# Thirty-two of forty-two projection blocks by seven products, with attention moved behind them

## The chip, the cores and the metric

The kernel runs on one core of one Trainium2 chip. The core has TensorE (PE, with a queue of its own for weight loads, PEld), VectorE (DVE), ScalarE (ACT), GpSimd (POOL) and SyncE (SP), which here issues nearly all DMAs. The metric is the time of one execution on the device in microseconds. A profile is one execution taken apart by the hardware profiler. Line numbers (L216) are those of the kernel file.

## The reference: what is computed

One layer of a decoder for 1024 prompt rows and 32 sample rows (8 sequences of 4), width 1024, all in float32:

```python
h = layer_norm(ALPHA * x + 0.5 * swiglu(x, f1_w1, f1_w3, f1_w2), ln1_g, ln1_b)
z = h @ w_in + b_in                       # 1024 -> 5376: q, k, v (3 x 768), u, v (2 x 512), gates (2 x 1024)
...
for g, (window, dil) in enumerate(ATT_GROUPS):   # (128,1), (512,4), (2048,16), 4 heads of 64 each
    o, lse, nbuf = dilated_attn_prompt(qg, kg, vg, tab, window, dil)      # or ..._sample with the stored keys
att = combine_groups(outs, lses).astype(h.dtype)          # softmax over the three groups' lse
yb, vrows = sgu_branch(uv, sgu_ln_g, sgu_ln_b, sgu_ws, sgu_b)   # gelu, LN of v, 128x128 token mixing, u * mixed
mix = (jax.nn.sigmoid(ga) * (att @ w_oa) + jax.nn.sigmoid(gb) * (yb @ w_ob)) @ w_out
h = layer_norm(ALPHA * h + mix, ln2_g, ln2_b)
h = layer_norm(ALPHA * h + 0.5 * swiglu(h, f2_w1, f2_w3, f2_w2), ln3_g, ln3_b)
```

Besides the rows of h it returns the last keys and values of each group (prompt and sample) and the normalised v rows of the sample.

## The kernel before

Everything stands transposed: features on the 128 partitions, the 1056 rows (1024 + 32) along the free dimension, in `NC` = 4 chunks of `C` = 264. Weights come as blocks of 128 output features. Each float32 operand is split into a rounded part and a rest (`split`, L227 a cast on ACT, L228 a subtraction on DVE), and each product is three matmuls (`mm3`, recorded at L216). A dense block for one chunk (`dense8`) is 8 x 3 = 24 matmuls of 128x128 by 264 columns.

The kernel's stages are: the first half step (`ffn`), `project`, `mix`, the second half step. In a half step most blocks are not computed densely. `hidden` takes two weight blocks as a 2x2 matrix of halves (two blocks, two halves of the 1024 inputs) and the rows as a 2x2 matrix (two halves of the inputs; even and odd chunks), and gets the product by seven products of sums and differences (the Winograd form of Strassen's scheme) instead of eight. `spread` makes the sums of the rows (four for each pair of chunks, on DVE, with casts on ACT), `prep` those of the weights (four additions on POOL or DVE, then splits), `product` runs the 24 matmuls of one of the seven. The results add up in three pairs of PSUM banks (`banks`).

`project` computes the 26 blocks of q, k, v and of the two SGU halves densely, in the order `ZORDER`. The first three blocks run chunk by chunk, as the first layer norm delivers its chunks; each result stays in SBUF. With every third block a head pair of one group is complete, and its attention (`attend`) is put in a queue. `attend` transposes v, forms scores (L1055), adds the bias and finds the row's limit (L1063, DVE), takes exponentials with their sums (L1067, ACT), transposes them (L1078, copied by ACT at L1082) and multiplies with v (L1094). The stored keys and values of the sample are worked on by DVE in slabs of 16 positions (`sample`, L1233 to L1250). `combine` weights the three groups by way of DRAM (L1154 to L1182, tables mlD and cD). SGU follows (`sgu_norm`, `sgu_mix`). `mix` computes the 16 gate blocks (sigmoid, L1393), the products with w_oa and w_ob (`product` inside it, L1402), their sum (L1409), and then w_out (L1491).

The order of work is set by the program and by a planner that fixes each engine's order before the run. Three queues of generators hold work that runs in between: `bg`, `slow`, `mid`. `tick(n, m)` lets n steps of `bg`, m of `slow` and three of `mid` into the program after each block; `step` takes always the first generator of its queue. `urgent` moves PSUM reads ahead. `STEPS` holds the numbers of steps for each stage. SBUF is given out in slots: 37 of 4.1 KB per partition (`S`), 8 for split weights (`W`), 2 for raw weights (`R`), 6 small ones (`M`). PSUM has three banks `mm` and five `ax`. A tile waits until a slot of its kind is free.

Of the kernel before, what the change touches and what calls it, by code (L numbers as in the profile page):

```python
# [20 lines left out]
P = 128  # L21
D = 1024
# [28 lines left out]
PIECE = 16  # L51
# [3 lines left out]
STEPS = dict(lead=6, strassen=3, seven=2, out=2, project=2, gate=1, wout=3)  # L55
# [10 lines left out]
ZORDER = [s * 6 + 2 * g + hp for hp, g in HPG for s in range(3)] + [22, 23, 24, 25] + [18, 19, 20, 21]  # L66


class Trunk:
# [705 lines left out]
    def out(self, w2, i, mode, ready, between, load):  # L775
# [84 lines left out]
        for c in range(NC):  # L860
            early = 6 if c == 0 else 0
            if mode != "out":
                self.hold_normed(c)
                if c == 2:
                    self.early = [self.unit(self.a["wz"][n], slot=True, ahead=AFTER) for n in range(3)]
                    self.early = self.early, [self.held([P, NT]) for _ in range(3)]
# [55 lines left out]
    def project(self):  # L922
        nc = self.nc
        self.att = [None, None]
# [4 lines left out]
        self.jD = self.dp.tile([6, 64, 66], F32, name="jD")  # L929
        lns, self.lns = self.lns, {}  # L930
        self.A = self.normed
        ws, held = self.early
        tiles = dict(enumerate(held))
        load = lambda i: self.unit(self.a["wz"][i])
        self.vr = [None] * 4
        self.vn = None
        self.yb = [None] * 4

        def block(i, w, c):
            if c in lns:  # L940
                self.drain(lns.pop(c))
            nb = ZORDER[i]
            p = self.mm_tile()[:, :C]
            self.dense8(p, w, c)
            if i not in tiles:
                tiles[i] = self.S([P, NT])
            t = tiles[i]
            ctx = self.urgent()
            ctx.__enter__()
            b, sc, dil = self.bin(nb), 1.0, 1  # L950
            if nb < 18:
                s, g = nb // 6, (nb % 6) // 2
                if s == 0:
                    b, sc = self.qb[:, nb : nb + 1], -0.125
                dil = GROUPS[g][1]
            put = lambda o, x: nc.scalar.activation(o, x, AF.Identity, bias=b, scale=sc)  # L956
            c0, c1 = c * C, c * C + C
            if dil == 1:
                put(t[:, c0:c1], p)
            else:  # L960
                cut = min(c1, NP)
# [7 lines left out]
                if cut < c1:  # L969
                    put(t[:, NP:], p[:, cut - c0 :])  # L970
# [709 lines left out]
```

## Time and profile before

| | us |
|---|---|
| median of 3 runs (2200.23 to 2209.55) | 2204.38 |
| the profiled execution's own time | 2201.41 |
| its span, first to last instruction | 2199.5 |
| TensorE busy in it | 2168.9 |
| DVE busy | 1467.2 |
| ACT busy | 869.1 |
| POOL busy | 254.7 |

The granted TensorE clock was 0.996 of full speed over the span. In a row of instruction groups stand: line, engine, operation, written tile <- read tiles, form, count; then busy time in us and mean ns of one; then idle time of the engine before them and who ended it. The busy time of a group counts overlapping instructions once, so it may be smaller than count times mean. In a row of stretches stand the window, its length and each engine's busy time with the number of instructions that began in it.

### The profile page before, as it was taken

To read this page: it belongs to the slowest core of one execution; us is meant where nothing else is said; L and a number is where in the kernel's file an instruction comes from. 1 tells how busy PE (TensorE), PEld (TensorE's weight loads), DVE (VectorE), ACT (ScalarE), POOL (GpSimd) and SP (SyncE) were. 2 spreads that over 40 slices of the span, in tenths; PEclk is the share of its full clock that TensorE was granted. 3 is DMA by queue.
4 is the path that set the end of the run, shared out by engine and by line. 5 is a ranking of instruction groups with operands and counts; after the bars stand their busy time and mean duration, and the time that the engine had idled before them with its cause. 6 is when DMAs were issued, how large, how long until landed. Compare 5 with 4: busy or idle time off the path is not lost.

```text
span 2199.5 us, 42970 instructions
## 1 busy us (share of the span) xinstructions
PE 2168.9 (99%) x17593; PEld 2125.4 (97%) x17593; DVE 1467.2 (67%) x2465; ACT 869.1 (40%) x1647; POOL 254.7 (12%) x193
## 2 busy tenths in 40 slices
PE   9999999999999999999999999999999999999997
PEld 8999999999999999888999999998999999999997
DVE  8776776656789337557862624578677667656787
ACT  5444444421125544444354123246444444322124
POOL 0432332200000000000000000000333233100000
PEclk9999999999999999999999999999999999999999
DMA  4445445596954135344531312513545445596832
GB/s 158 146 139 179 171 161 183 186 378 258 348 205 155 69 103 184 96 155 157 195 109 68 111 48 79 180 69 112 175 156 185 171 159 178 197 366 250 313 103 80
DMA packets 136278, 370.33 MB, mean 168 GB/s; under 512 B 21056, under 2 KB 48432, under 8 KB 133392
## 3 DMA queue, kind: packets, MB, share of 16 engines
q1 hardware_dynamic: 135648, 367.04, 48.1%
q8 instruction: 138, 2.26, 0.4%
q10 hardware_dynamic: 432, 0.54, 0.1%
q14 instruction: 60, 0.49, 0.1%
HBM read 277.85 MB, written 135.86 MB: 188 GB/s over the span
## 4 chain that ended last, share of the span: by engine, by line
PE 92%; DVE 3%; DMA 2%; ACT 1%; issue 1%; ACTq 0%; SPq 0%; DVEq 0%
PE mm L216 49%; PE ax L216 39%; PE ax L1055 1%; PE ax L1094 1%; PE ax L1078 1%; DVE S L228 1%; DMA S<-kv 1%; DVE S L594 0%; DMA S<-cD 0%; PE ax L1361 0%; DMA S<-xc 0%; PE ax L583 0%; ACT S L227 0%; ACT S L602 0%; DVE S L523 0%
## 5 line engine op out<-in xcount | busy, mean ns | idle before, releaser
L216 PE MATMUL mm<-S,W 128*128 128x264 f32 x7224 | 936.7, 287 | 9.4 <-DVE S L858 4.9
L216 PEld LDWEIGHTS mm<-S,W 128*128 128x128 f32 x7224 | 899.6, 189 | 25.1 <-issue 11.0
L216 PE MATMUL ax<-S,W 128*128 128x264 f32 x4536 | 596.0, 284 | 0.0
L216 PEld LDWEIGHTS ax<-S,W 128*128 128x128 f32 x4536 | 570.0, 188 | 1.0 <-issue 1.0
L216 PE MATMUL ax<-S,S 128*128 128x264 f32 x2664 | 390.9, 285 | 0.0
L216 PEld LDWEIGHTS ax<-S,S 128*128 128x128 f32 x2664 | 351.2, 188 | 1.0 <-DVE S L228 0.6
L216 PE MATMUL mm<-S,S 128*128 128x264 f32 x2184 | 334.9, 286 | 4.7 <-ACT S L227 2.8
L216 PEld LDWEIGHTS mm<-S,S 128*128 128x128 f32 x2184 | 294.3, 189 | 6.3 <-ACT S L227 3.2
L227 ACT CAST W<-R 128x1024 fp32r<-128x1024 f32 (+4 forms) x177 | 139.8, 806 | 383.8 <-PE mm L216 171.1
L228 DVE TENSOR_TENSOR W<-R,W 128x1024 fp32r<-128x1024 f32 (+4 forms) x177 | 163.7, 931 | 83.0 <-ACT W L227 82.8
L770 DVE SCALAR_TENSOR_TENSOR S<-ax,S 128x264 f32<-128x264 f32 x240 | 100.0, 431 | 64.2 <-PE ax L216 63.8
L433 DVE TENSOR_TENSOR S<-ax,M 128x264 f32<-128x264 f32 x84 | 33.6, 433 | 154.4 <-PE ax L216 154.4
L95 POOL CAST S<-ones 128x1 fp32r<-128x1 f32 x32 | 12.6, 423 | 988.9 <-PE mm L216 733.5
L358 POOL TENSOR_TENSOR Q<-R 128x512 f32<-128x512 f32 x38 | 53.5, 1408 | 569.8 <-DMA R<-w13b 229.8
L227 ACT CAST S<-Q 128x1024 fp32r<-128x1024 f32 (+2 forms) x74 | 72.6, 983 | 102.3 <-PE ax L216 71.5
L228 DVE TENSOR_TENSOR S<-Q,S 128x1024 fp32r<-128x1024 f32 (+2 forms) x74 | 108.0, 1459 | 6.5 <-ACT S L227 5.6
L227 ACT CAST W<-Q 128x1024 fp32r<-128x1024 f32 (+1 forms) x66 | 64.1, 971 | 114.6 <-DVE Q L359 67.7
L228 DVE TENSOR_TENSOR S<-S,M 128x528 fp32r<-128x528 f32 x72 | 84.0, 1166 | 3.8 <-ACT M L227 2.3
L228 DVE TENSOR_TENSOR W<-Q,W 128x1024 fp32r<-128x1024 f32 (+1 forms) x66 | 74.5, 1129 | 6.5 <-ACT W L227 6.5
L956 ACT ACTIVATE S<-mm,cols 128x264 f32<-128x264 f32 (+5 forms) x104 | 46.9, 496 | 77.8 <-PE mm L216 74.5
L438 DVE TENSOR_TENSOR S<-S,M 128x264 f32<-128x264 f32 x84 | 52.1, 621 | 34.1 <-ACT S L437 30.4
L227 ACT CAST S<-R 128x512 fp32r<-128x512 f32 (+1 forms) x52 | 36.4, 703 | 91.3 <-DMA sumsA<-S 40.3
(199 smaller groups left out, 1982.2 us busy)
## 6 DMA issues: line engine op xcount, KB each, us to landing
ws<-st SPq DMA_DIRECT2D x144, 256.0 KB
S<-sumsA SPq DMA_DIRECT2D x63, 528.0 KB
S<-sumsB SPq DMA_DIRECT2D x63, 528.0 KB
S<-kv SPq DMA_DIRECT2D x48, 512.0 KB
sumsA<-M SPq DMA_DIRECT2D x90, 264.0 KB
sumsB<-M SPq DMA_DIRECT2D x90, 264.0 KB
R<-w13b SPq DMA_DIRECT2D x44, 512.0 KB
R<-w13a SPq DMA_DIRECT2D x42, 512.0 KB
```

The source lines that it names most:

```text
L95: self.nc.gpsimd.tensor_copy(t[:, 0, :1] if len(shape) == 3 else t[:, :1], self.ones[:, :1])
L216: mm = lambda a, b, s, e: nc.tensor.matmul(o, a[:, cc], b, start=s, stop=e, skip_group_check=True)
L227: a = self.nc.scalar.copy(hi, src)
L228: b = self.nc.vector.tensor_tensor(lo, src, hi.bitcast(F32), op=ALU.subtract)
L358: tt(s12[:, lo], cd[:, lo], cd[:, hi], op=ALU.add)
L433: go(one, 5, False, lambda x: tt(h[:, x, 1], one[x], p7[:, x], op=ALU.add))
L438: lambda x: tt(h[:, x, 0], h[:, x, 0], r1[:, x], op=ALU.mult),
L770: nc.vector.scalar_tensor_tensor(y(x, r, e), bank[x], HALF, y(x, r, e), op0=ALU.mult, op1=ALU.add)
L956: put = lambda o, x: nc.scalar.activation(o, x, AF.Identity, bias=b, scale=sc)
L1055: nc.tensor.matmul(pS[h][:, r, :nk], q[e, i * P : (i + 1) * P], k[e, k0 : k0 + nk], start=True, stop=True)
L1078: nc.tensor.transpose(pT[r][:, h, o], s[:, r, h, o], self.ident)
L1094: nc.tensor.matmul(pv[0][e, (i % 4) * P : (i % 4 + 1) * P], V[:, i - (nb - 1) + b, e], sT[:, r, h, b * P : b * P + P], start=b == 0, stop= ...
```

## The change

Of the 42 blocks of w_in, 32 are now computed by seven products in 16 pairs (`pair`, run by `widen` in place of `project`): q, k and v in the order in which attention wants them (9 pairs), the two SGU halves (4 pairs) and 6 of the 16 gates (3 pairs). Ten gates stay dense: two chunk by chunk behind the layer norm, four more as a lead while the sums of the rows are made, and four in `mix`. Every result goes to a DRAM table `zD`, and is fetched again by who needs it.

Attention and SGU no longer run between the projections. They stand in `bg` and `mid` at the start of `mix`; the four last gates (4 blocks x 4 chunks) run among them with 5 steps of `bg` each, then the products with w_ob for the first four output blocks (2 steps each), and then what is left of the queues. For the gates in `mix`, two halves of the normed rows that were given up are fetched and split again (`again`). Only the sample's slab work starts earlier: it is queued behind pairs 2, 5 and 8 and runs one step per product, in slabs of 8 positions that lie in three `M` tiles; its values are laid out by the host so that the sum runs over neighbouring elements. The merge of the two branches, the split for w_out and the running sum work on whole blocks of 1056 rows.

```diff
-STEPS = dict(lead=6, strassen=3, seven=2, out=2, project=2, gate=1, wout=3)
+STEPS = dict(lead=6, strassen=3, seven=2, out=2, tail=5, wob=2, wout=3)
...
-PIECE = 16
+PIECE = 8
+SLABS = 3
...
+NLEAD = 6
+NTAIL = 4
+CHUNKED = 2
+SPLIT = [*QKV, 22, 23, 24, 25, 18, 19, 20, 21, *GATES[NLEAD : 16 - NTAIL]]
+DENSE = GATES[:NLEAD] + GATES[16 - NTAIL :]
+NZ = len(SPLIT) // 2
...
+    def gate8(self, w, nb, c, *steps):
+        nc = self.nc
+        p = self.mm_tile()[:, :C]
+        self.dense8(p, w, c)
+        t = self.M([P, C])
+        with self.urgent():
+            nc.scalar.activation(t, p, AF.Sigmoid, bias=self.bin(nb))
+        nc.sync.dma_start(self.zD[nb][:, c * C : c * C + C], t)
+        self.tick(*steps)
...
+    def pair(self, f, between):
...
+        a, c = lin(ta, n1), lin(tc, n2)
+        go(one, 1, True, put(one, a, 0))
+        go(two, 2, True, add(two, a, 0), *([lambda x: sig(ta, x, 0, 1)] if gate else []))
+        go(one, 6, False, put(one, c, 0))
+        go(three, 7, True, put(three, c, 1))
+        go(one, 5, False, add(one, c, 1))
+        go(three, 4, False, add(three, c, 0), *([lambda x: sig(tc, x, 0, 2)] if gate else []))
+        self.send(tc, n2)
+        go(one, 3, False, put(one, a, 1, AF.Sigmoid if gate else AF.Identity))
+        self.send(ta, n1)
+        if n1 < 18:
+            self.bg.append(self.sample_rows((n1, ta), (n2, tc)))
+            if f % 3 == 2:
+                self.slow.append(self.sample(f // 3))
...
+    def widen(self):
...
+        self.slow.append(self.spread(0, Y, self.A, nc.vector))
         for c in range(NC):
...
+            self.drain(lns.pop(c))
+            if c == NC - 1:
+                self.slow.append(self.spread(1, Y, self.A, nc.vector))
+            for n in range(CHUNKED):
+                self.gate8(units[n], DENSE[n], c, STEPS["lead"], 1)
...
+        for f in range(NZ):
+            for _ in preps.pop(f):
+                pass
+            if f < NZ - 1:
+                begin(f + 1)
...
+            self.pair(f, between)
+            del self.L[f]
...
-        yield
+        yield from self.pause(2)
+        self.fetch_qkv(i + 1)
...
+        def local(n):
+            wb = self.unit(a["wo"][n, :, 2 * P :], 4 * P)
+            mt[n] = self.fetch_z(34 + n)
+            for c in range(NC):
+                product(wb, self.yb, c, mt[n])
+                self.tick(STEPS["wob"], 1)
+
+        self.A = self.again([[None if c % 2 and j == 0 else self.normed[c][j] for j in range(2)] for c in range(NC)])
...
+        sgu = [self.sgu_norm()] + [self.sgu_mix(gg) for gg in range(4)]
+        self.mid.extend(sgu)
+        self.bg.extend(self.attend(i) for i in range(len(HPG)))
+        units = [self.unit(a["wzp"][NLEAD + n]) for n in range(NTAIL)]
+        for c in range(NC):
+            for n in range(NTAIL):
+                self.gate8(units[n], DENSE[NLEAD + n], c, STEPS["tail"], 1)
+        units = self.A = None
+        while any(g in self.mid for g in sgu):
+            self.step(self.mid, 1)
+        for n in range(KB // 2):
+            local(n)
         self.drain()
         split_att()
...
         for n in range(KB):
...
+            wa, ta = self.unit(a["wo"][n], 2 * P), self.fetch_z(26 + n)
+            if n < KB // 2:
+                local(KB // 2 + n)
             for c in range(NC):
...
+                product(wa, att, c, ta)
+                self.tick(2)
+            nc.vector.tensor_tensor(mt[n], mt[n], ta, op=ALU.add)
+            m2.append((self.S([P, NT], F32R), self.S([P, NT], F32R)))
+            self.split(*m2[n], mt[n])
             done += 1
```

321 lines of the change are left out of this document (154 added, 167 removed).

## The prediction

> **What bounds the kernel now.** I read the page first: the busy line, then the chain of work that ended last.
>
> ```profile
> span 2199.5 us, 42970 instructions
> PE 2168.9 (99%) x17593; PEld 2125.4 (97%) x17593; DVE 1467.2 (67%) x2465; ACT 869.1 (40%) x1647; POOL 254.7 (12%) x193
> ...
> PE 92%; DVE 3%; DMA 2%; ACT 1%; issue 1%; ACTq 0%; SPq 0%; DVEq 0%
> ```
>
> TensorE is busy 99% of the span and is 92% of the chain, so time can only be won by fewer or denser matmuls. Then I cut the span into stretches; the columns are the busy time of PE, PEld, DVE, ACT and POOL, the granted clock, the DMA share and GB/s.
>
> ```profile
> 25.00:50.00 25.00, 25.00 (x208) 25.00 (x208) 24.48 (x27) 15.65 (x23) 0.00 (x0) 1.00 0.21 59
> 300.00:325.00 25.00, 25.00 (x208) 25.00 (x207) 18.78 (x23) 10.20 (x19) 11.21 (x8) 1.00 0.52 174
> 450.00:475.00 25.00, 25.00 (x208) 25.00 (x207) 11.78 (x25) 5.14 (x10) 0.00 (x0) 1.00 1.03 398
> 650.00:675.00 25.00, 20.89 (x148) 19.56 (x147) 21.69 (x35) 9.89 (x15) 2.08 (x7) 0.94 0.58 193
> 675.00:700.00 25.00, 24.61 (x199) 24.26 (x199) 23.11 (x43) 13.81 (x28) 0.00 (x0) 1.00 0.24 86
> 725.00:1050.00 325.00, 322.63 (x2587) 292.18 (x2586) 173.06 (x354) 155.09 (x412) 0.00 (x0) 1.00 0.40 128
> 1050.00:1125.00 75.00, 75.00 (x618) 74.47 (x617) 62.31 (x90) 39.75 (x62) 0.00 (x0) 1.00 0.48 159
> ```
>
> A full stretch holds 208 matmuls in 25 us: 0.120 us for each. That is so in the first half step's seven products (300 to 325), with DVE at 98% (25 to 50) and with DMA at 398 GB/s (450 to 475). The same form of rows for the lines of the matmul helper alone shows how many of them lie in the attention stretch:
>
> ```profile
> 725.00:1050.00 325.00, 250.79 (x1897) 236.03 (x1896) 1.00 0.40 128
> 1050.00:1125.00 75.00, 72.08 (x580) 70.74 (x579) 1.00 0.48 159
> 1525.00:1900.00 375.00, 375.00 (x3086) 375.00 (x3085) 1.00 0.49 166
> ```
>
> 1897 of them at 0.120 us are 228 us of 325; the other 97 us are what attention costs TensorE, waits and changes of operand included. In dense pieces of the chain its kinds take less:
>
> ```profile
> 768.76 1.02 PE ax L1078 x8
> 769.78 1.07 PE ax L1055 x8
> 773.95 1.07 PE ax L1094 x16
> ```
>
> 140 transposes, 192 score and 280 value matmuls at these prices are 18 + 26 + 19 = 63 us, about 70 with the small ones: some 27 us of the 97 are friction.
>
> **What is saved.** A dense pair of blocks is 2 x 4 chunks x 24 = 192 matmuls; seven products of 4 x 2 x 3 = 24 are 168. Sixteen pairs save 16 x 24 = 384. At 0.120 us that is **-46.2 us**, at the slower 375 us row (375/3086 = 0.1215) -46.7; I take -46.2. Nothing else takes matmuls away: ten blocks stay dense, and attention, SGU and the three later products keep theirs.
>
> **The start.** Between the layer norm's steps there are now two blocks per chunk instead of three (24 matmuls less cover each), and their sigmoids alternate with the norm's square roots. The old start lost 416 - 148 - 199 = 69 matmuls, 8.3 us. Two blocks less cover and two or three function loads of 1.3 us (below) against a later deadline of the rest: +2, between -2 and +7. The sums and differences of the seven operands are 16 subtractions of about the 1.23 us shown below, 20 us of DVE, beside 16 casts on ACT; the four other lead gates (384 matmuls, 46 us) hide them. Without that cover the first product would wait up to 20 us.
>
> **The seven-product stage.** A pair is 168 x 0.120 = 20.2 us. The weights' preparation is the one of the first half step: same queue order, four POOL additions. On DVE a pair has that preparation, six additions out of PSUM, and seven slab steps of the sample attention, which moves here.
>
> ```profile
> L228 DVE TENSOR_TENSOR S<-Q,S 128x1024 fp32r<-128x1024 f32 (+2 forms) x74 | 108.0, 1459 | 6.5 <-ACT S L227 5.6 <-PE ax L216 0.6
> L1233 DVE TENSOR_TENSOR S<-S,X 128x1024 f32<-128x1024 f32 (+1 forms) x27 | 30.6, 1134 | 23.7 <-DMA S<-kv 23.5
> L1402 DVE TENSOR_TENSOR S<-S,mm 128x264 f32<-128x264 f32 x32 | 13.4, 426 | 9.2 <-PE mm L216 9.2
> L206 SPq DMA_DIRECT2D R<-wz x26: 327/333/1352, 659.9 to 1045.1; - x26
> ```
>
> 3.5 splits x 1.46 + 6 x 0.43 + 7 steps of two half-size (0.6 us) operations = 5.1 + 2.6 + 8.4 = 16.1 us of 20.2, 80%; the first row of the stretches ran at 98% and PE did not stall. The dilated groups cut an addition into up to four pieces: up to 2 us more per pair. Per pair SP issues about 2 weight loads, 2 results, up to 2 window outputs, 7 slabs, 2 state copies and a few small rows, some 20 x 0.33 = 7 us of 20. They move 1.0 + 1.1 + 1.8 + 0.5 to 1.0 + 0.5 MB, about 5 MB in 20 us: 250 GB/s, under the 398 that cost nothing. A result waits in SP for the last ACT or DVE write of its block, with the next weights' load behind it; those are asked for a pair ahead. I take +2 us, between 0 and +20. In all, 42 blocks of 528 KB go out and come back, 45 MB on 370; the dense gates' quarter results too leave by SP.
>
> **The attention stage.** Behind the last pair TensorE has four gates (384 matmuls, 46 us), the attention (97 us), SGU (12 us: the 618 - 580 foreign matmuls of 1050 to 1125 and their like later) and four of the local products (4 x 48 matmuls, 23 us): 178 us. Four more local products need no attention, but the weight pool of 8 lets about three be issued ahead, 17 us. ScalarE's load there, all its lines of one attention stretch first (the row is the exponentials with their accumulator reads and one load):
>
> ```profile
> 710.00:1130.00 420.00, 47.15 (x193) 1.00 0.42 137
> ...
> L1082 ACT COPY S<-ax 128x256 f32<-128x256 f32 (+1 forms) x48 | 21.9, 471 | 20.2 <-PE ax L1078 19.8
> L1105 ACT COPY S<-ax 128x512 f32<-128x512 f32 x8 | 8.5, 1058 | 7.5 <-PE ax L1094 7.5
> L1036 ACT COPY Q<-ax 128x512 f32<-128x512 f32 x12 | 7.1, 594 | 3.3 <-PE ax L1035 3.3
> L1337 ACT ACTIVATE S<-S,X 128x512 f32<-128x512 f32 (+1 forms) x9 | 6.7, 803 | 0.0
> L1353 ACT ACTIVATE S<-S 128x1056 f32<-128x1056 f32 x4 | 4.3, 1087 | 0.0
> L1325 ACT COPY S<-ax 128x512 f32<-128x512 f32 (+1 forms) x9 | 4.8, 589 | 0.3 <-PE ax L1323 0.3
> L227 ACT CAST S<-M 128x512 fp32r<-128x512 f32 x8 | 4.9, 616 | 11.0 <-DVE M L1374 11.0
> ```
>
> 46 + 22 + 8.5 + 7 + 2 = 86 us for attention; SGU 6.7 + 2 x 4.3 (gelu of both halves) + 4.8 + 5 of splits and small ones = 26; 16 sigmoids of 0.48 (below) are 8; eight casts of weights and reloaded operands, about 1 us each, 8: 128 us. To it come the loads of function tables:
>
> ```profile
> 1159.83 0.48 ACT L1393 ACTIVATE S<-mm,cols 128x264 f32<-128x264 f32 x1
> 1160.34 1.28 ACT L1269 ACT_TABLE_LOAD   x1
> 1161.63 0.30 ACT L1269 ACTIVATE X<-M,X 128x3 f32<-128x3 f32 x1
> 1161.94 1.28 ACT L1393 ACT_TABLE_LOAD   x1
> 1163.24 0.48 ACT L1393 ACTIVATE S<-mm,cols 128x264 f32<-128x264 f32 x1
> ```
>
> Sigmoid, exponential, sigmoid cost two loads of 1.28 us. Before, the sigmoids all came after the exponentials of the scores. Now the 16 gates lie among them, a gate for every one to two blocks of scores, so up to 32 loads, and some 9 more for gelu, square root and the combinations: 41 x 1.28 = 52 us. ACT: 128 + 52 = 180, TensorE: 178. Two engines equally full do not mesh perfectly; I take +8 us idle on TensorE, between 0 and +50 (every load on the path). The friction of 27 us can also shrink, since attention's matmuls now stand closer together: below nothing, to -15.
>
> The Trainium skill, ScalarE: Activation LUTs, section What ACT_TABLE_LOAD costs, says that a switch costs 1283 ns and about 1380 ns of draining besides, 2.66 us. In the rows above the activation starts 0.01 us behind its load and the load 0.03 us behind the activation before, so the trace shows the first part alone. By the page ACT would hold 128 + 41 x 2.66 = 237 us, an estimate, and the kernel would end some 50 us later than I forecast, so slower than before.
>
> **The end of attention.** The last combination (softmax weights of the three groups) used to run beside gates. Now it ends the stage:
>
> ```profile
> 904.34 3.30 DMA cD<-S
> ...
> 908.32 3.99 DMA S<-cD
> ...
> 912.40 1.23 DVE S L1179
> ```
>
> Two round trips ahead at the 3.3 us of the write: 6.6; DVE and ACT on 16 rows about 6; the write 3.3; three broadcasts one behind the other (one buffer) 12; five multiplications and additions 6.2; the split of the result 2.3: 36 us. The three local products cover 17, and it begins some 4 us before the last values end: **+15 us**, between 0 (more local work left) and +30.
>
> **The merge and w_out.** For the last four blocks TensorE has only 24 matmuls, 2.9 us, while DVE has four multiplications (0.43), an addition and a split of 1.25 each, the running sum (1.32) and a weight split:
>
> ```profile
> L1442 DVE SCALAR_TENSOR_TENSOR S<-S,X,S 128x1056 f32<-128x1056 f32 x7 | 9.2, 1315 | 0.1
> ```
>
> 5.8 us each, so 4 x 2.9 = 12 us short, of which the first w_out blocks take about half ahead, three banks of them: +6, between 0 and +18. Everything behind is untouched.
>
> **Sum.** On the profiled execution's own time of 2201.4 us, which is 3.0 under the median of 2204.4: -46.2 + 2 + 2 + 8 + 15 + 6 = -13 us, so 2188 there and **2191 us** against the median.
>
> **Rivals.** (1) *ScalarE becomes the bound, and the kernel is slower.* Place: the 16 gates among the exponentials. Each sigmoid holds up the next exponential by 3 us, and TensorE's order, which is fixed, stands behind the transposes that wait for it. Price: all 52 us of loads on the path instead of 8: 2191 + 44 = 2235. It decides as soon as about 21 us, 16 of the 41 loads, fall where TensorE has nothing it may do (then nothing is won). For it: 180 against 178 us. Against it: 63 us of dense work lie ready in the same stage, and gates that come before the first exponential need no load. (2) *DVE in the seven-product stage is late.* If strided additions and slab steps cost half more, 22 us stand against 20.2 in the dozen pairs that hold slabs: +20, 2211, about as before. Against it: the full DVE at 25 to 50. (3) *All is covered:* friction shrinks by 10 and the combination finds its cover: 2191 - 8 - 15 - 5 = 2163. For it: samples, with their 2 us reductions, no longer stand in DVE's queue before the score rows. (4) *The saving does not come,* because preparation or results hold up each pair: that would show as under 208 matmuls in 25 us; the first half step, with the same preparation, speaks against it.
>
> **How the numbers follow.** Forecast 0.32, (3) 0.13, (2) 0.17, (1) 0.30, a mixture of late ends 0.08. 0.5% (11 us) is about what a measurement of this kernel tells from no change: faster 0.45 (forecast and (3)), same 0.17, slower 0.38. The forecast's own range is 2172 to 2210; with both signs in, 2157 to 2239, leaving out the worst of (1) and the best of (3).
>
> **What would show it.** Some 384 matmuls of the helper fewer; 208 per 25 us in the pairs; about 40 table loads between the last pair and the last scores, with TensorE near full there; a stretch of some 15 us with little TensorE work ahead of the first products of the attention result. The forecast falls if TensorE idles over 25 us before the last scores, or if pairs take over 21 us.

## The result and the profile after

The changed kernel takes 2308.95 us (median of 4), the kernel before 2206.38 in the same session: 1.0468 times as long, 95% interval 1.0442 to 1.0494. I had forecast 2191 and a range of 2157 to 2239: the wrong side, and by more than any rival allowed. The profiled execution took 2307.2 us, its span is 2305.4.

First the page of the changed kernel, from its parts 1 and 2: engine totals, then busy tenths in 40 slices of 57.6 us each.

```profile
span 2305.4 us, 43046 instructions
...
PE 2164.4 (94%) x17209; PEld 2107.5 (91%) x17209; DVE 1576.9 (68%) x2722; ACT 935.5 (41%) x1713; POOL 339.0 (15%) x250
...
PE   9999999999998999999898864699999999999997
...
DVE  8777767566788337878535465658777777746787
ACT  5444444311136333423388830226444344421124
...
PEclk9999999999999999999997886899999999999999
```

17593 - 17209 = 384 matmuls are gone, exactly the number predicted. But TensorE, which was at 99%, is at 94%, and nearly all that it lost lies in slices 20 to 26, from 1095 to 1498 us. No other engine is full there: ScalarE is nearest, with 8 of 10 in three of them, and hardly works behind those. The granted clock of TensorE falls as well. From the first w_out block on the two kernels differ by under 3 us.

That is where the windows go (all matmuls, then those of the helper alone, which is line 224 here: lines have moved by 8 and more). After the interval and its length come busy time and count for PE, PEld, DVE, ACT and POOL, the granted clock, DMA share and GB/s.

```profile
775.00:1128.00 353.00, 346.58 (x2824) 344.54 (x2824) 235.82 (x381) 129.73 (x247) 81.26 (x58) 1.00 0.56 193
1128.00:1350.00 222.00, 188.42 (x1327) 149.07 (x1325) 106.18 (x366) 165.57 (x364) 0.00 (x0) 0.87 0.43 141
1350.00:1400.00 50.00, 17.08 (x118) 15.51 (x118) 24.92 (x56) 7.40 (x19) 0.00 (x0) 0.70 0.47 138
1400.00:1497.00 97.00, 66.43 (x420) 64.50 (x420) 61.52 (x92) 17.42 (x21) 3.65 (x10) 0.78 0.45 155
...
1128.00:1350.00 222.00, 84.58 (x572) 75.73 (x570) 0.87 0.43 141
1350.00:1400.00 50.00, 14.23 (x96) 14.03 (x96) 0.70 0.47 138
1400.00:1497.00 97.00, 66.43 (x420) 64.50 (x420) 0.78 0.45 155
```

Read against a full TensorE at 0.120 us a matmul, each stage shows its loss:

- The pairs, 775 to 1128: 353 - 2824 x 0.120 = 14 us.
- Attention, 1128 to 1350: 222 - 572 x 0.120 - 97 (attention at the price it had before, friction included) - 12 (SGU) = 44 us. TensorE is idle for 222 - 188.4 = 34 of them; the rest lies in matmuls that take longer, at a granted clock of 0.87.
- The end of attention, 1350 to 1400: 50 - 96 x 0.120 = 38 us.
- The merge, 1400 to 1497: 97 - 420 x 0.120 = 47 us.
- The start, 650 to 775, holds 873 matmuls: 125 - 105 = 20 us, where the old start lost 8: 12 more.

Together 155 us. From the end of the first feed-forward part (650 in both) to the first w_out block (its first multiplication and addition) it is 1388.8 - 650 = 738.8 us before and 1497.3 - 650 = 847.3 after: 108.5 longer, and with the 46.2 saved, 154.7 have been lost. The stages account for about the whole of it; that the sums agree to a microsecond is chance, since the small matmuls among them are priced only roughly.

Next the changed kernel's waits of TensorE from 1128 to 1500 (engine, instruction's line, releaser: us in all, times, longest), and TensorE's timeline through the merge (start, length, group; in brackets the idle time before it).

```profile
PE mm L224 <- DVE S L1491: 59.1, 9, 24.4
PE ax L1168 <- ACT S L1157: 18.8, 8, 6.7
PE ax L1125 <- DMA S<-zD: 6.2, 1, 6.2
...
1358.12 14.23 PE L224 MATMUL mm<-S,W 128*128 128x264 f32 x96 [5.45 <-DVE S L1491]
1376.41 0.30 PE L1376 MATMUL ax<-ident,X 128*128 128x128 f32 x1 [4.06 <-DVE X L1373]
1401.10 10.73 PE L224 MATMUL mm<-S,W 128*128 128x264 f32 x72 [24.39 <-DVE S L1491]
1418.73 11.70 PE L224 MATMUL mm<-S,W 128*128 128x264 f32 x72 [6.89 <-DVE S L1491]
1435.59 11.80 PE L224 MATMUL mm<-S,W 128*128 128x264 f32 x72 [5.16 <-DVE S L1491]
```

L1491 is the multiplication that takes a product out of PSUM onto its gate; TensorE waits until it has emptied a bank. VectorE comes late to it for two different reasons. Here are VectorE's waits from 1340 to 1500, three rows of its timeline, and SyncE's own queue:

```profile
DVE S L1491 <- DMA S<-zD: 24.2, 6, 7.3
...
DVE S L1271 <- DMA S<-cD: 8.3, 4, 3.4
...
DVE S L1269 <- DMA S<-cD: 5.0, 1, 5.0
...
1399.36 1.23 DVE L236 TENSOR_TENSOR S<-S,S 128x1024 fp32r<-128x1024 f32 x1 [1.01 <-ACT S L235]
1400.62 1.11 DVE L1491 TENSOR_TENSOR S<-S,mm 128x264 f32<-128x264 f32 x3
...
1418.24 1.11 DVE L1491 TENSOR_TENSOR S<-S,mm 128x264 f32<-128x264 f32 x3 [5.49 <-DMA S<-zD]
...
1379.54 12.77 SPq L1264 DMA_DIRECT2D S<-cD  x6
1392.35 1.06 SPq L1083 DMA_DIRECT2D S<-zD  x2
...
1410.68 1.06 SPq L1083 DMA_DIRECT2D S<-zD  x2
```

TensorE's longest wait, 24.4 us up to 1401, is the last combination: VectorE waits 5.0, 3.4 and 3.3 us for its broadcast weights (cD), multiplies, adds, splits the result, and comes to the multiplication at 1400.6, with no wait for a gate right before it. Inside the merge behind it the gate (zD) is what VectorE waits for: five waits of up to 5.5 us there, 16.9 of the 24.2 us. The gates lie in DRAM and are asked for two at a time, when their block is already due. The first two stand behind the six broadcasts of the combination, which hold SyncE's queue for 12.8 us; the next two are issued 18 us later, behind loads of weights. 72 matmuls, 8.6 us at full clock, come every 17 us.

### The profile page after: what moved, and what is told of

It reads as the page before. It is cut to its first block, busy times and chain, and to the rows that moved or that the text cites. A ratio compares the mean times of both kernels' runs of the same rounds, so it can differ in the third digit from the quotient of the medians.

```text
span 2305.4 us, 43046 instructions
## 1 busy us (share of the span) xinstructions
PE 2164.4 (94%) x17209; PEld 2107.5 (91%) x17209; DVE 1576.9 (68%) x2722; ACT 935.5 (41%) x1713; POOL 339.0 (15%) x250
## 5 line engine op out<-in xcount | busy, mean ns | idle before, releaser
L224 PE MATMUL ax<-S,W 128*128 128x264 f32 x5688 | 743.0, 284 | 0.6 <-ACT S L975 0.6
L224 PEld LDWEIGHTS ax<-S,W 128*128 128x128 f32 x5688 | 712.7, 188 | 2.3 <-ACT S L975 1.2
L224 PE MATMUL mm<-S,W 128*128 128x264 f32 x4632 | 638.7, 294 | 72.1 <-DVE S L1491 59.1
L224 PEld LDWEIGHTS mm<-S,W 128*128 128x128 f32 x4632 | 605.6, 196 | 84.8 <-DVE S L1491 61.2
L224 PE MATMUL ax<-S,S 128*128 128x264 f32 x3432 | 505.4, 285 | 0.5 <-DVE S L984 0.5
L224 PEld LDWEIGHTS ax<-S,S 128*128 128x128 f32 x3432 | 453.6, 188 | 1.9 <-DVE S L984 0.7
L235 ACT CAST W<-R 128x1024 fp32r<-128x1024 f32 (+3 forms) x170 | 125.8, 756 | 427.0 <-PE mm L224 195.8
L236 DVE TENSOR_TENSOR W<-R,W 128x1024 fp32r<-128x1024 f32 (+3 forms) x170 | 148.1, 878 | 20.7 <-ACT W L235 20.6
L367 POOL TENSOR_TENSOR Q<-Q,R 128x512 f32<-128x512 f32 x53 | 87.6, 1652 | 2.7
L374 POOL TENSOR_TENSOR Q<-R,Q 128x512 f32<-128x512 f32 x53 | 86.5, 1633 | 1.4
```

The source lines that it names most:

```text
L224: mm = lambda a, b, s, e: nc.tensor.matmul(o, a[:, cc], b, start=s, stop=e, skip_group_check=True)
L235: a = self.nc.scalar.copy(hi, src)
L236: b = self.nc.vector.tensor_tensor(lo, src, hi.bitcast(F32), op=ALU.subtract)
L367: tt(s12[:, hi], s12[:, lo], ab[:, lo], op=ALU.subtract)
L374: tt(s34[:, hi], ab[:, hi], s12[:, hi], op=ALU.subtract)
```

## The experiments

Each run is timed beside the kernel before. Runs of different sessions are compared by their ratio to it; 0.001 of the ratio is 2.2 us. No kernel leaves out work.

### Fetching the gates ahead

```diff
+        want = deque([34, 35, 36, 37] + [x for n in range(4) for x in (26 + n, 38 + n)] + [30, 31, 32, 33])
+        def gate_of(nb):
+            while want and (nb not in here or len(here) <= ZAHEAD):
+                m = want.popleft()
+                here[m] = self.fetch_z(m)
+            return here.pop(nb)
...
-            wa, ta = self.unit(a["wo"][n], 2 * P), self.fetch_z(26 + n)
+            ta = gate_of(26 + n)
+            wa = self.unit(a["wo"][n], 2 * P)
```

> The gates kept in DRAM are fetched four tiles ahead of their use, and ahead of the weights in program order. Theory (the merge waits for tiles whose fetch stands late in SP's queue, behind weight loads and the broadcasts of the last combination): the merge from 1400 to 1500 us shrinks to 55 to 65 us and some local products move into the empty stretch before it, so about 2309 - 50 = 2260 us. Rival (the merge is bound by DVE's whole-block work and the running sum): it keeps 85 us or more, 2295 to 2309.

Measured: 2281.57 us, ratio 1.0351 (1.0331 to 1.0371), 26 us less than the changed kernel by the ratios. The late fetch was worth more than half of the merge's 47 us: in this trace VectorE waits for no gate between 1340 and 1500, and the first w_out block comes at 1468.3 in place of 1497.3. The hole ahead of the merge stays; in this kernel's timeline (helper on line 225) TensorE now waits there for the splits of the attention result and stands in front of the blocks behind them:

```profile
1380.00 1.03 PE L225 MATMUL mm<-S,W 128*128 128x264 f32 x3 [13.14 <-ACT S L236]
1389.60 1.69 PE L225 MATMUL mm<-S,W 128*128 128x264 f32 x6 [8.56 <-DVE S L237]
1402.95 1.03 PE L225 MATMUL mm<-S,W 128*128 128x264 f32 x3 [11.67 <-ACT S L236]
1404.21 19.87 PE L225 MATMUL mm<-S,W 128*128 128x264 f32 x144 [0.23 <-DVE S L237]
```

### The sigmoids taken out of the attention

```diff
-                self.gate8(units[n], DENSE[NLEAD + n], c, STEPS["tail"], 1)
+                self.gate8(units[n], DENSE[NLEAD + n], c, STEPS["tail"], 1, fn=AF.Identity)
...
+            else:
+                nc.scalar.activation(ta, ta, AF.Sigmoid)
```

> The four gates among the attention are stored without their sigmoid; it is applied to the fetched block in the merge. Theory (the alternation of sigmoid and exponential fills ScalarE): some 29 of 37 table loads go, 37 us of ACT, and the stretch from the last pair to the last scores (222 us) gets 20 to 35 us shorter: 2275 to 2290 us. Rival (the stretch is bound by the chain scores, limit, exponential, transposition, whatever ACT's load): under 8 us shorter, over 2300.

Measured: 2290.27 us, ratio 1.0389 (1.0365 to 1.0412), 17 us less. The table loads of both kernels between 1128 and 1400, the changed kernel first:

```profile
L1157 ACT ACT_TABLE_LOAD x16 | 20.5, 1283 | 0.3
L935 ACT ACT_TABLE_LOAD x13 | 16.7, 1283 | 1.5 <-issue 1.3
```

```profile
L1157 ACT ACT_TABLE_LOAD x8 | 10.3, 1283 | 0.1
L1449 ACT ACT_TABLE_LOAD x4 | 5.1, 1283 | 0.1
```

With the small groups the loads go from 37 to 15 (41 were predicted). 22 loads of 1.28 us are 28 us of ScalarE; the time fell by 17, about 0.6 of each load. By the traces the last values come 10 us earlier, at 1342 in place of 1352; the rest is won behind the attention. In the changed kernel ScalarE was busy 165.6 of 222 us and TensorE 188.4: neither was full, and a load still cost time, since the next exponential, the transposes behind it and TensorE's fixed order all stood behind it. The Trainium skill, ScalarE: Activation LUTs, section What ACT_TABLE_LOAD costs, has 2.66 us for a switch with its draining, which would be 58 us of ScalarE for 22 of them, an estimate. The end of the kernel moved by 17 us, less than the 28 us of the loads alone.

### Three broadcast tiles, and the start's sums later

```diff
-        cb = self.S([P, NP])
         for g in range(3):
+            cb = self.S([P, NP])
```

> Each group's weights get a broadcast tile of their own instead of one for all three. Theory (the three broadcasts follow each other, 4 us each, and hold SP's queue with the fetches behind them): the empty stretch before the merge gets 8 to 12 us shorter, 2295 to 2301 us. Rival (the weights' own way through DRAM sets it): within 4 us of 2309.

Measured: 2305.59 us, ratio 1.0463 (1.0437 to 1.0489): nothing that these four runs, 2299 to 2313, can tell. In the trace the six broadcasts hold SyncE's queue for 3.7 us in place of 12.8, and from the second combination's reciprocal to the first products of the merge it is 19 us in place of 24; but in this execution the reciprocal itself came 4 us later. So what the one buffer costs, 12 us of my 36, stays open. The first gates of the merge were asked for 5 us earlier, and that shows no gain either.

```diff
-        self.slow.append(self.spread(0, Y, self.A, nc.vector))
         for c in range(NC):
...
             if c == NC - 1:
+                self.slow.append(self.spread(0, Y, self.A, nc.vector))
```

> The sums of the first chunk pair's rows start behind the last layer norm step instead of before the first. Theory (they take DVE and ACT from the norm of the last chunk, where TensorE then waits 9 us): 6 to 9 us shorter, 2300 to 2303 us. Rival (the smaller cover, two gates per chunk, is what lacks): within 3 us of 2309, or longer where the first pair then waits for the sums.

Measured: 2310.35 us, ratio 1.048 (1.0463 to 1.0496): nothing, and this was odd, since in its own stage the edit won: 569 matmuls in the 75 us up to 775, where the changed kernel has 548. The 2.5 us were gone again by the end of attention. The same with the next edit.

### The row transposes later

```diff
     def sample_rows(self, *blocks):
...
-        yield
+        yield from self.pause(4)
```

> The changed kernel with one edit: the row transposes of the sample attention stand four pieces of dense work behind the copies they read, not one. Nothing is left out. Theory: TensorE's waits for those copies in the pairs (5.4 us in all) go, and the time falls by 5 to 8 us, to about 2302. Rival: the wait is taken over by the next step of the pairs, and the time stays within 3 us of 2308.

Measured: 2312.03 us, ratio 1.0497 (1.047 to 1.0524): nothing in the end either, though the pairs ran better, 2857 matmuls against 2824:

```profile
700.00:775.00 75.00, 71.19 (x569) 70.67 (x570) 53.32 (x73) 46.48 (x77) 1.06 (x3) 0.98 0.31 111
```

```profile
775.00:1128.00 353.00, 350.28 (x2857) 347.35 (x2856) 238.13 (x386) 131.99 (x252) 80.87 (x58) 1.00 0.56 194
```

The first row is of the kernel with the sums later, the second of this one. Their 2.5 and 4 us do not reach the end, so some wait behind them seems to set the end, and not TensorE's work ahead of it.

### All local products ahead of the last combination

Beside the earlier fetch:

```diff
-        for n in range(KB // 2):
+        for n in range(KB):
             local(n)
...
-            if n < KB // 2:
-                local(KB // 2 + n)
```

> The gate quarters are fetched ahead as in the run that did so alone (2281.57 us), and all eight products with the local half of the mixing matrix are placed ahead of the last combination, not the first four alone; nothing is left out. Theory: the hole of 23 to 35 us before the merge's first products is only a lack of work ready, so it takes the four products of 5.8 us (about 23 us) and the time falls to about 2258 (2253 to 2264). Rival: the combination's round trips also get later, since their preparation shares VectorE and ScalarE with the four products' weight splits, and the gain is below 8 us (2274 or more).

Measured: 2278.06 us, ratio 1.0337 (1.032 to 1.0355), 3 us by the ratios below the run that fetched ahead alone, which the intervals do not tell from zero: the rival. The four products did fill time ahead of the merge, but a hole of 12.75 us then stood behind them, up to 1412, and the first w_out block came at 1468.9 as against 1468.3: what was filled ahead was missing as cover inside the merge.

### Three mended parts, and ten gates beside the attention

The first of these two joins the earlier fetch, the late sigmoids (applied when the quarter comes back) and the local products. The second has ten gates beside the attention, so three pairs fewer, and lets 3 steps of attention in behind each block, not 5:

```diff
-STEPS = dict(lead=6, strassen=3, seven=2, out=2, tail=5, wob=2, wout=3)
+STEPS = dict(lead=6, strassen=3, seven=2, out=2, tail=3, wob=2, wout=3)
...
-NTAIL = 4
+NTAIL = 10
+ROUND = 4
...
+        for first in range(NLEAD, NLEAD + NTAIL, ROUND):
+            some = range(first, min(first + ROUND, NLEAD + NTAIL))
+            units = {n: self.unit(a["wzp"][n]) for n in some}
```

> As the run before it, and the four gates among the attention's scores are stored without their sigmoid, which is applied where their quarters come back. Nothing is left out. Theory: the parts add: 27 us for the earlier fetch, 17 for the sigmoids and some 20 for the local products, from 2308 to about 2243 (2236 to 2252). Rival: they share one wait (attention ending earlier only lengthens the hole behind it) and it stays above 2256. Either way it should stay slower than the kernel before (2204).

> As the run before it, but thirteen pairs instead of sixteen go by seven products, and ten dense gates instead of four lie among the attention; nothing is left out. It computes 72 matmuls more (8.7 us at 0.120) and has 69 us more of dense work beside attention. Theory: attention lacks dense work beside it, the 50 us lost there shrink to under 20, and the time is 20 to 40 us below the run with three mended parts (about 2210). Rival: the attention's chain through ScalarE and VectorE sets its length, the added gates only lengthen it, and the time is 0 to 9 us above that run.

Measured: 2262.89 us, ratio 1.0277 (1.0258 to 1.0296), and 2255.68 us, ratio 1.0234 (1.0219 to 1.025). The three mends give 42 us by the ratios (alone 26, 17 and 3), not the 65 expected of them. Ten gates, with 72 matmuls more to do, save 7 us more, not 20 to 40: between the two expectations. Attention begins 70 us earlier now and its last values come 52 us earlier (1299 and 1351). The chain behind it did not follow. Three rows of the changed kernel show why (a line's instructions: count, shortest, median and longest ns, first and last start): the sample attention's last reduction, the reciprocal of each combination, and the weight loads of the value matmuls.

```profile
L1342 DVE TENSOR_REDUCE X<-M x48: 609/677/687, 927.5 to 1337.0; 128x64 f32<-128x512 f32 x45, 128x64 f32<-128x256 f32 x3
...
L1253 DVE RECIPROCAL X<-X x2: 941/941/941, 1347.6 to 1376.6; 16x128 f32<-16x128 f32 x2
...
L1184 PEld LDWEIGHTS ax<-S,Q x280: 132/137/232, 1166.6 to 1352.3; 128*64 128x64 f32 x140
```

The values end at 1352, yet both combinations come at the very end, 29 us apart, the first straight behind the sample attention. In the kernel with ten gates it is the same more clearly: values end at 1299, the sample attention at 1317, the reciprocals come at 1325 and 1355. Both kinds of step stand in one queue, served from its front, one step per dense block.

### The order and the pace of the queue of slow steps

```diff
         if g == 2:
-            self.slow.append(self.combine(hp))
+            self.slow.appendleft(self.combine(hp))
```

on the changed kernel, on the kernel with ten gates, and on that with four local products back in the merge:

> The changed kernel with one edit: the combination of the three groups goes ahead of the sample attention in the queue of background steps in which both stand, not behind it. Nothing is left out. In all runs so far the two combinations came one behind the other, the first some 10 us after the last step of the sample attention (1337.0, reciprocal 1347.6) and the second 29 us later (1376.6), though the last values end at 1352. Theory: this order sets the end of attention; the first combination moves to the middle of the attention, the second's reciprocal to about 1364, and the time falls by 8 to 14 us, to about 2297. Rival: the second combination is held by its own round trips and by the same engines, its reciprocal stays within 4 us of 1376, and the time stays within 4 us of 2308.

> The run with ten gates beside attention (2255.68), with the same edit. There the last values end at 1299 and the second combination's reciprocal comes at 1355. Theory: the combinations end before the local products do (1360), the holes of 12 and 4 us before the merge go, and the time falls by 14 to 20 us, to about 2238. Rival: the merge, in which VectorE is full for 50 us, takes the gain, and the fall is below 6 us.

> As the run before it, but with four of the eight local products back among the merge's blocks, as in the changed kernel. Nothing is left out. Theory: the merge's eight blocks are bound by VectorE (about 7 us each against 2.9 us of TensorE), so four products of 5.8 us lie free there, and with the combinations early there is no hole to fill ahead of it: 8 to 14 us below the run before it. Rival: the weight splits of the four products go to the same VectorE, or the hole ahead of the merge opens again, and the time is within 5 us of that run or above it.

Measured: 2310.99 (1.0484, 1.0465 to 1.0503), 2259.24 (1.0251, 1.0234 to 1.0268) and 2265.41 us (1.029, 1.0267 to 1.0312). The theory fell all three times. With ten gates the combinations did move (reciprocals at 1220.5 and 1308.2), but now the sample attention came last, its end at 1376 instead of 1317, and TensorE stood in front of the transpose that takes its result. That wait in the second and the third kernel:

```profile
PE ax L1378 <- DVE X L1375: 17.9, 1, 17.9
```

```profile
PE ax L1378 <- DVE X L1375: 29.5, 1, 29.5
```

In these kernels the order in the queue only chooses which end is late. The next edit, on the same three kernels, changes its pace:

```diff
-                self.gate8(units[n], DENSE[NLEAD + n], c, STEPS["tail"], 1)
+                self.gate8(units[n], DENSE[NLEAD + n], c, STEPS["tail"], 2)
...
-                self.tick(STEPS["wob"], 1)
+                self.tick(STEPS["wob"], 2)
```

> The changed kernel with one edit: the queue of slow steps (sample attention, then the combinations) takes two steps per dense gate block beside attention and per local product, not one. Nothing is left out. Theory: the queue's rate of one step per dense block ends the attention stage: the sample attention ends before 1290 (before 1337.0), the first combination follows it, the second one begins when its values are there (reciprocal near 1364, before 1376.6), and the time falls by 8 to 14 us to about 2297. Rival: the queue is not the limit, or its steps on VectorE hold up the score rows as much, and the time stays within 4 us of 2308.

> The run with ten gates and the combinations first (2259.24), with two slow steps per dense block. There the sample attention ended at 1376 and TensorE then stood 17.9 us at the transpose behind it. Theory: the sample attention ends before 1330, that wait goes, and the time falls by 14 to 18 us to about 2243. Rival: the merge behind it, with VectorE full, takes the gain: a fall below 6 us.

> The same edit on the run with four local products back in the merge (2265.41, where TensorE stood 29.5 us at that transpose). Theory: the wait goes, and the products lie beside VectorE's work in the merge: a fall of 25 to 32 us to about 2236, below the run before it. Rival: their weight splits lengthen VectorE's work in the merge, and it stays level with the run before it or above.

Measured: 2303.59 (1.0464, 1.0433 to 1.0494), 2240.35 (1.0168, 1.0149 to 1.0187) and 2231.91 us (1.0133, 1.0109 to 1.0157). With ten gates the edit is worth 18 and 35 us by the ratios, a little more than expected: there the pace of that queue ended the stage, and the local products in the merge are 8 us better than ahead of it. In the changed kernel it is worth nothing that these runs can tell from zero. Its rows, again the last reduction, the reciprocals and the values:

```profile
L1342 DVE TENSOR_REDUCE X<-M x48: 590/677/687, 929.3 to 1251.1; 128x64 f32<-128x512 f32 x45, 128x64 f32<-128x256 f32 x3
...
L1253 DVE RECIPROCAL X<-X x2: 941/941/941, 1270.4 to 1367.6; 16x128 f32<-16x128 f32 x2
...
L1184 PEld LDWEIGHTS ax<-S,Q x280: 132/136/232, 1165.8 to 1356.7; 128*64 128x64 f32 x140
```

The sample attention ends 86 us earlier, the second combination 9 us, the values 4 us later. With four gates the attention itself is the late one: 11 us lie between its last value and the reciprocal, and 36 us between that value and the merge's first products at 1393. My queue theory therefore holds for the kernels with ten gates and falls for the changed kernel. One rival is left there: these runs on the changed kernel still fetch the gates late, and TensorE's last wait is again ended by the multiplication by a gate. The last run below has the fetch mended too.

### Is VectorE the merge's bound?

```diff
-            nc.vector.tensor_tensor(mt[n], mt[n], ta, op=ALU.add)
+            nc.gpsimd.tensor_tensor(mt[n], mt[n], ta, op=ALU.add)
```

> As the run before it, and the merge's eight additions of the two halves (1.25 us each on VectorE, 10.1 us in all) go to GpSimd. Theory: VectorE is the merge's bound, and the time falls by 5 to 9 us more. Rival: GpSimd takes about 3.3 us for each (1.6 us for 512 columns in the preparation of the seven products), lies in the chain from product to split, and the time stays or rises by up to 8 us.

Measured: 2235.4 us, ratio 1.0141 (1.0123 to 1.0159), which the intervals do not tell from the run before it: the rival. GpSimd takes 2.95 us where VectorE took 1.25, and the addition lies in the chain from product to split. So this run does not tell how much VectorE's load costs in the merge.

### Start and pairs once more, the first fetches, and four gates with every mend

On the best kernel so far (ten gates, two slow steps, four local products in the merge), first the two edits at the start and in the pairs that had given nothing alone, then

```diff
             units = {n: self.unit(a["wzp"][n]) for n in some}
+            while first + ROUND >= NLEAD + NTAIL and len(here) < 3:
+                m = want.popleft()
+                here[m] = self.fetch_z(m)
```

and, as the third run, that best kernel without these edits, with four gates and sixteen pairs again (and, as in the changed kernel, 5 steps of attention behind each gate block).

> The best run so far (2231.91: ten gates beside attention, two slow steps per block, four local products in the merge) with the two edits that gave nothing when made alone on the changed kernel: the operand sums after the last norm, and the sample attention's row transposes four pieces later. Nothing is left out. In their own stages they won about 21 matmuls (2.5 us) and 33 matmuls (4 us). Theory: they gave nothing then because the slow queue ended the attention whatever TensorE did; with that limit gone they come through: 5 to 8 us less, about 2225. Rival: what they win is lost elsewhere again (a wait on the same copies, the next stage's weights): within 2 us of 2232.

> As the run before it, and three gate quarters of the local products are fetched before the last round of dense gates. In the best run so far TensorE stood 6.4 us at 1320 because the first of them was asked for at 1322.98, behind stores that wait in SP's queue. Theory: 5 to 7 us less than the run before it. Rival: the fetched blocks hold three slots that attention's tiles then wait for, and the time rises.

> As the best run so far (2231.91) but with the changed kernel's own sixteen pairs and four dense gates beside attention: 72 matmuls fewer (8.7 us). Nothing is left out. Theory: with the queue mended, what remains is that attention has too little dense work beside it; with four gates only, TensorE idles some 20 to 35 us more in it, and the time is 12 to 26 us above 2232 (2244 to 2258). Rival: the queue was the whole matter and sixteen pairs are then worth their 8.7 us: about 2223.

Measured: 2227.92 (1.0096, 1.0077 to 1.0115), 2220.26 (1.0058, 1.004 to 1.0075) and 2262.32 us (1.0257, 1.0241 to 1.0274), beside 2206.87 for the kernel before in that session. By the ratios the start and the pairs give 8 us (4 by the medians of the two sessions), so that here at least part of what they win comes through, and the early fetch another 8. Four gates cost 27 us against ten, a little more than expected, though they have 8.7 us less to compute: TensorE loses 36 us more where dense work is missing. Windows of the kernel with ten gates (first fence) and of that with four, then TensorE's timeline of the latter behind its last values:

```profile
1250.00:1300.00 50.00, 50.00 (x388) 40.02 (x387) 13.31 (x70) 30.45 (x97) 0.00 (x0) 1.00 0.23 74
1300.00:1350.00 50.00, 43.37 (x331) 42.11 (x331) 24.77 (x58) 15.79 (x25) 0.00 (x0) 0.93 0.64 219
```

```profile
1200.00:1250.00 50.00, 40.70 (x296) 31.84 (x295) 22.55 (x91) 39.14 (x105) 0.00 (x0) 0.85 0.33 107
1250.00:1300.00 50.00, 42.59 (x299) 31.39 (x297) 29.70 (x96) 35.89 (x87) 0.00 (x0) 0.83 0.58 183
1350.00:1400.00 50.00, 25.38 (x171) 23.55 (x171) 32.55 (x65) 7.68 (x14) 0.00 (x0) 0.69 0.51 166
...
1371.02 1.69 PE L225 MATMUL mm<-S,W 128*128 128x264 f32 x6 [10.22 <-DVE S L237]
1383.90 1.03 PE L225 MATMUL mm<-S,W 128*128 128x264 f32 x3 [11.20 <-ACT S L236]
1385.16 19.86 PE L225 MATMUL mm<-S,W 128*128 128x264 f32 x144 [0.23 <-DVE S L237]
```

With four gates TensorE has holes through the attention (ScalarE 36 to 39 of 50 us) and half a stage empty behind it. From the last pair to the last values it is idle for 26 of 225 us, with ten gates for 11 of 230. Counted with matmuls of 0.120 us, some 17 of the 36 us lie there and some 17 behind the last values: there the chain of the last combination takes 32 us, from 1353 to 1385, with few products left to cover it, although the gates are fetched ahead and the queue of slow steps is ahead of time (reciprocals at 1259 and 1361). With ten gates the longest wait behind the last values is 6.4 us. The two kernels differ in the steps of attention behind each block as well; no run varies these alone.

No version beats the kernel before: the best is 0.6% slower (0.4 to 0.75), having 312 matmuls, 37 us, less to do. So it loses some 50 us more than the kernel before: 9 at the start (125 - 902 x 0.120 = 17, where the old one lost 8), and the rest in the pairs, among the attention and in the merge. Which waits these are was not tested.

## Why the prediction was wrong

**The saving** was right: 384 matmuls fewer, and 208 in 25 us where a pair runs undisturbed.

**The start**, +2 forecast, was 12. I had counted the sums of the operands (20 us of VectorE) as hidden by the four lead gates. They did hide them: the first pair begins at 795.7 without a wait. But VectorE and ScalarE work on the first of these sums among the last steps of the norm, and TensorE waited 4.8 us at 741 for the last normed chunk (shown in the last section), with two gates a chunk as cover. With the sums behind the norm that stage won 2.5 us; what the rest of the 12 is was not separated. Work that a cover hides still takes time on the engines that the step before it needs.

**The seven-product stage**, +2, was 14, inside the range given (0 to 20): 5.4 us are waits of the row transposes for the copies that ScalarE makes, another 1 us waits of the products, and for the rest the trace shows no wait. Over 16 pairs that is 0.9 us each, so about 21 us a pair on average, right at the limit that the prediction named as a sign against it. Rival 2, VectorE late in every pair, did not come: from 900 to 1125, with the slab steps running, there are 1772 matmuls, 197 in 25 us, but only 0.5 us of TensorE's waits were ended by VectorE.

**The attention stage**, +8, was 44, near the upper end of its 0 to 50, and this is the step that failed in kind. I set ScalarE's 180 us against TensorE's 178 and took a small misfit. Neither was full. Each block goes from scores to exponential to transposes to copies to values, one engine after the other, and TensorE keeps to a fixed order; what decides is how much dense work lies between the links. Before, 1897 helper matmuls, 228 us, lay in the attention's 325 us, and TensorE was idle for 2.4 of them; after the change 572, 69 us, lay in 222, and it was idle for 34, 18.8 of them at transposes that waited for exponentials. "Friction can also shrink, since attention's matmuls now stand closer together" had the sign wrong: closer together they wait for each other. The late sigmoids brought the last values 10 us forward, and ten gates in place of four give some 17 us in this stage; the 6.2 us that the first scores wait for their operands out of DRAM belong here too. What is left of the 44 us was not separated. Rival 1 named the right place and was too cheap; it priced the loads alone, and the loads were not the larger part.

**The end of attention**, +15, was 38. I counted one combination and three local products hoisted ahead of it. There were two combinations, both behind the sample attention in one queue. And the products that I counted as cover did not run ahead: with the gates fetched ahead TensorE still stood idle for 33 us, in three waits for the splits of the attention result, with the products behind these in its order. Which of the two decides depends on the kernel: with ten gates the pace of the queue does; with four neither its order nor its pace changes the time, since the chain behind the last value is long enough by itself (32 us with every mend, 36 in my sum), so there the missing cover decides.

**The merge**, +6, was 47: the largest miss. I priced VectorE and TensorE, and of the DMAs only their bytes. A gate that is kept in DRAM has to be asked for early enough, and here each was asked for when its block was due, behind the broadcasts of the combination and behind loads of weights in SyncE's queue. Fetching ahead gave back 26 us. How much of that is the broadcasts is open: with them at 3.7 us in place of 12.8 the time did not move. Another 16 of the 47 us are matmuls that ran slower behind waits (last section). I had said of the queue in the pairs that what waits there is asked for a pair ahead; I did not ask the same question here.

The sum of these errors is 10 + 12 + 36 + 23 + 41 = 122 us: 2188 + 122 = 2310 against the profiled 2307. The statement that the forecast falls if TensorE idles over 25 us before the last scores was met, with about 34. One slip is in the prediction's own sums: rival 3 takes off 5 us for a friction that its sentence puts at 10; nothing else rests on it.

## What to carry to other kernels

When work is moved to the front of a program, what it used to cover is left bare. List, for the stages that it leaves, the chain from engine to engine, and count the independent work that lies between its links; two engines that are 85% and 75% full, as TensorE and ScalarE were here, can both wait. A result that is put in DRAM needs its own line in the sum for when its fetch is issued and what stands ahead of it in that queue; and background steps given out at a fixed rate per block of dense work can be what ends a stage, as they were here with ten gates.

## What the runs showed of the hardware

I had priced every matmul at 0.120 us. Behind a wait it is dearer. The changed kernel in its start stage, behind the last steps of the norm:

```profile
741.26 0.81 PE L224 MATMUL mm<-S,S 128*128 128x264 f32 x2 [4.78 <-ACT S L235]
741.87 4.68 PE L224 MATMUL mm<-S,W 128*128 128x264 f32 x24
746.39 5.80 PE L224 MATMUL mm<-S,S 128*128 128x264 f32 x46
```

After 4.8 us of idling 24 matmuls take 0.195 us each, the 46 behind them 0.126. In the merge, with a wait of 5 to 7 us ahead of each group of 72, a matmul takes 11.7 / 72 = 0.163 us, and the granted clock of the stage is 0.78. There 66.4 us of busy time hold what 50.4 would at full clock: 16 of the merge's 47 us are slow matmuls, not idle time. The Trainium skill, TensorE: Matmul & The Clock Gate, section What's actually happening, says that an idle window of about 3.4 us puts the clock at half, and a busy one of about the same length back at full. The rows agree in direction: waits of 5 us and more are followed by slow groups, while in the best kernel ahead of the two last edits (2231.91 us) the waits of the merge are 3 us and less and the clock of its 50 us windows stays at 0.90 to 1.00. The border is not sharp in them: behind a wait of 3.0 us in that merge 18 matmuls took 3.14 us, 0.174 each. So a stall costs its length and, at 741, 24 x (0.195 - 0.120) = 1.8 us more. Whether splitting one wait into short ones is worth something in itself, no run here measured.
